# Sample projections of a hybrid layer: later column matmuls, row sums through DRAM and VectorE, spatial weights transposed one step later

## The chip, the cores and the metric

The kernel runs on one core of a Trainium2 chip. The metric is the device time of one execution in microseconds (us); the time of a kernel is the median of its runs. Each run is one whole step of the layer, from the inputs in device memory to all nine outputs there.

## What is computed

One decoder layer is applied to two groups: a prompt of 2048 tokens, and eight samples of one new token each, with their stored state. Both go through one input projection with 3856 columns, whose column groups feed three mixers: sliding-window attention (A), a chunked spatial gating unit (B) and gated linear attention (C). The mixers' outputs are gated, joined and projected back.

```python
h = rmsnorm(x, g_norm)
proj = h @ w_in_l                    # (T, 1024) @ (1024, 3856)
(qa, ka, va, ga, ub, vb, gb, qc, kc, vc, gc, lr) = split(proj)
ya = attention(qa, ka, va)           # window 128, bias, sinks; samples use stored keys
yb = ub * (spatial_w @ layernorm(vb) + spatial_b)   # in chunks of 128 tokens
yc = gla(qc, kc, vc, decay(lr))      # recurrent state per head
y = concat([ya * silu(ga), yb * silu(gb), yc * silu(gc)])
x = x + y @ w_out_l
```

The eight samples need the same `h @ w_in_l` with eight rows; this change concerns how those eight rows are made and handed on. The last keys and values of the prompt, the new keys and values of the samples, the recurrent states and the normalised `vb` rows of the samples are outputs too.

## The kernel before, in words

**Numbers and passes.** The f32 operands of the large products are split into two f16 halves (hi and lo), and each product is three f16 passes (hi hi, hi lo, lo hi) summed in PSUM.

**Stages.** The prompt is cut into 8 chunks of 256 tokens (16 tiles of 128). Stage A runs the A columns over all chunks with the attention beside them, stage B the B columns with the spatial mixing, stage C the C columns with the gated linear attention, and stage F the output projection. A *unit* is one accumulation of 24 matmuls (8 k-steps by 3 passes) into a PSUM bank of the tag `pp`: `mm_col` (L296) gives columns by tokens, `mm_tok` (L307) tokens by columns. There are four `pp` banks for units and four `mx` banks for everything else. The final projection's units have 36 matmuls (L1008).

**What a unit feeds in stage A.** Gate units: ACT writes a tanh (L486), DVE multiplies it with the bank (L487). Query units: ACT writes the hi half (L476), DVE the lo half (L477). Key and value units the same way (`unit_va` around L457). In the last chunk `unit_k` also makes the output of the last 128 keys: DVE scales the bank into `kf` (L441), PE transposes it (L443), ACT copies it and SP stores it.

**Attention beside the units.** A step is a tile and half of the heads: score matmuls (L506), DVE's bias-and-maximum (L510), small DVE steps (L520 to L524), ACT's exponentials (L538), an f16 copy by ACT (L548) into the tile `pha` and a subtraction by GpSimd (POOL, L549) into `phb`, small DVE steps (L551 to L558), two DMA transposes on SP into `pt` (L563), the products with the values on PE (L578), two DVE multiplications (L583, L585) and a store on SP (L588). Tiles `pha` and `phb` have one buffer each, the tag `yy` has six, `pt` two.

**Splitting the weights.** A slice of 512 columns is loaded by SP (L164), ACT writes the hi half, DVE the lo half (L204). The slices for stage B are split in stage A.

**The order.** Steps are emitted in the order of a clock: every k-step of a unit advances `now` by its columns divided by 2400 (so about the us at full clock), and `at(t, f)` puts a step on a list that runs when `now` reaches t. `weave`, `merge` and `spread` place steps between the units of stages B, C and F. On top of this the Tile framework's scheduler chooses each engine's order; it has to hold what is written by one engine and read by another, and what `tc.keep_in_program_order` names.

**A sample projection** (`sample_proj`, L322) takes one slice of the weights. 16 matmuls (`four_way`, L320) of 32 columns by up to 512 fill four groups of 32 partitions; each group holds partial sums of hi and lo parts for the eight samples. ACT copies the bank, scaled, to the `yy` tile `part` (L329). The eight partial sums of each sample (four groups, hi and lo rows of `h`) must still be added, which a matmul with the selector `selg` (128 x 8, f32) does in two forms:

- *columns* (calls with `keep`, A0 and C0, and the 16 low-rank columns of A1): `part` is the stationary operand, so the result lies columns on partitions (L334, L338); DVE copies it to `scolA`, `scolC` or `slr` (L336, L339);
- *rows* (calls with `outs`): `selg` is the stationary operand (L343); ACT copies the 8 rows (L345) and SP stores them to the DRAM tile `sp_d` (L347), from which the sample steps of the mixers read much later (`sA_load`, `sC_load`, whose loads are at L1187 among others, and the output at L1045).

The calls: A1 (rows for keys and values, columns for the low rank), A0 (columns), A2 (rows) near the end of stage A, eight units of clock apart; B0, B1, B2 (rows) in chunk 2 of stage B; C0 (columns), C1, C2 (rows) in chunk 1 of stage C.

**Spatial weights.** `consts_B` (L593) runs in the last slots of chunk 0 of stage B. SP loads the weights of eight groups into `pha` and `phb` (L601), PE transposes them (L609), DVE masks them, and PE transposes the biases (L613). The first reader is `b_mix`, in chunk 1.

Other lines the text refers to: L904, a DVE reduce of stage C; L942, a load of output weights by SP in stage C.

Of the kernel before, what the change touches and what calls it, by code (L numbers as in the profile page):

```python
# [10 lines left out]
F32 = mybir.dt.float32  # L11
# [5 lines left out]
ALU = mybir.AluOpType  # L17
AX = mybir.AxisListType
# [21 lines left out]
DIN = _o  # L40
# [3 lines left out]
def hybrid_step_kernel(ctx: ExitStack, tc: tile.TileContext, I, O):  # L44
    nc = tc.nc
    V, S, G, PE, SP = nc.vector, nc.scalar, nc.gpsimd, nc.tensor, nc.sync
# [33 lines left out]
    def mbank():  # L80
        return psm.tile([128, 512], F32, tag="mx", name=nm("mx"))
# [7 lines left out]
    def w4(tag, shape, dt=F32):  # L89
        return wk.tile(shape, dt, tag=tag, name=nm(tag), bufs=WB.get(tag, 2))  # L90
# [3 lines left out]
    hs_d = dr.tile([16, DM], F16, name="hs_d")  # L94
    ys_d = dr.tile([16, DMIX], F16, name="ys_d")
    sp_d = dr.tile([NB, DIN], F32, name="sp_d")

    w_in = I["w_in"][0]
    w_out = I["w_out"][0]
# [176 lines left out]
    def at(t, *fs):  # L276
        for f in fs:
            cnt[0] += 1
            bisect.insort(EV, (t, cnt[0], f))
# [42 lines left out]
    def sample_proj(name, n, outs, keep=None):  # L322
        w = SL[name]
        inv = INVI[name]
        m = n % 128
        ps = mbank()
        four_way(ps, min(n, 512), lambda i: hs[:, i // 2, :], [w[:, i % 2, i // 2, 0:n] for i in range(16)])
        part = w4("yy", [128, 512])
        S.activation(out=part[:, :n], in_=ps[:, :n], func=AF.Copy, scale=inv)  # L329
        if keep is not None or m:  # L330
            p2 = mbank()
            cols = range(n // 128) if keep is not None else ()
            for ct in cols:
                PE.matmul(p2[:, ct * 8:ct * 8 + 8], part[:, ct * 128:(ct + 1) * 128], selg, start=True, stop=True)  # L334
            if keep is not None:
                V.tensor_copy(out=keep.rearrange("p a b -> p (a b)"), in_=p2[:, 0:32])  # L336
            if m:
                PE.matmul(p2[:m, 32:40], part[:, n - m:n], selg, start=True, stop=True)  # L338
                V.tensor_copy(out=slr, in_=p2[:m, 32:40])  # L339
        if outs:  # L340
            p3 = mbank()
            nf = n - m
            PE.matmul(p3[:8, :nf], selg, part[:, :nf], start=True, stop=True)  # L343
            row = w4("yy", [8, 512])
            S.copy(row[:, :nf], p3[:8, :nf])  # L345
            for a, b, off in outs:
                SP.dma_start(out=sp_d[:, off:off + b - a], in_=row[:, a:b])  # L347

    BM = {}

# [242 lines left out]
    def consts_B():  # L593
        t = one.tile([128, 2048], F32, tag="bm", name="phB")
        wsT["w"] = t[:, 0:1024].rearrange("p (a b) -> p a b", a=8)
        wsT["g"] = t[:, 1024:1536]
        wsT["b"] = t[:, 1536:2048]
        wsT["bs"] = sm.tile([128, 8], F32, tag="bs", name="bs", bufs=1)
        ws = [w4("pha", [128, 4, 128]), w4("phb", [128, 4, 128])]
        for q in range(2):  # L600
            SP.dma_start(out=ws[q], in_=I["spatial_w"][0, 4 * q:4 * q + 4].rearrange("h i j -> i h j"))  # L601
        SP.dma_start(out=wsT["g"], in_=I["chunk_ln_g"].partition_broadcast(128).rearrange("p a b -> p (a b)"))
        SP.dma_start(out=wsT["b"], in_=I["chunk_ln_b"].partition_broadcast(128).rearrange("p a b -> p (a b)"))
        bsr = small([8, 128])
        SP.dma_start(out=bsr, in_=I["spatial_b"][0])
        for q in range(2):
            ps = mbank()
            for i in range(4):
                PE.transpose(ps[:, i * 128:(i + 1) * 128], ws[q][:, i, :], ident)  # L609
            V.tensor_tensor(out=wsT["w"][:, 4 * q:4 * q + 4, :], in0=ps.rearrange("p (a b) -> p a b", a=4),  # L610
                            in1=upm.unsqueeze(1).to_broadcast([128, 4, 128]), op=ALU.mult)
        ps = mbank()
        PE.transpose(ps[:, 0:8], bsr, ident[:8, :8])  # L613
        V.tensor_copy(out=wsT["bs"], in_=ps[:, 0:8])
# [670 lines left out]
    def merge(*seqs):  # L1285
        n = max((len(s) for s in seqs), default=0)
        out = [[] for _ in range(n)]
        for s in seqs:
            for i, fs in enumerate(s):
                out[i * n // len(s)] += fs  # L1290
        return out

    def spread(steps, at, total):
        out = [[] for _ in range(total)]
        for s, i in zip(steps, at):
            out[min(i, total - 1)].append(s)
        return out

    if True:
# [88 lines left out]
        for c in range(NCH):  # L1388
            units = [unit_vb(c, 0), unit_vb(c, 1), unit_gate("B1", hgB, c, 0), unit_gate("B1", hgB, c, 1),
                     unit_ub(c, 0), unit_ub(c, 1)]  # L1390
            extra = []
            if c == 0:
                for f, d in zip(prB[2][1:], (0, 9, 10.5, 12)):
                    at(now[0] + d, f)
                V.tensor_scalar(out=hgB, in0=INVI["B1"], scalar1=0.5, scalar2=None, op0=ALU.mult)
                side = [[]] * 11 + [[lambda: V.tensor_scalar(out=cB, in0=hgB, scalar1=INVI["B2"], scalar2=None, op0=ALU.mult),
                                     consts_B]]
            else:
                side = mixB(c - 1)
            if c == 1:  # L1400
                extra = spread([sA_load, sA_kT], [1, 4], 6)
            if c == 2:
                extra = spread([sA_soft, sA_pv,
                                lambda: sample_proj("B0", 512, [(0, 512, OFF["vb"])]),
                                lambda: sample_proj("B1", 512, [(0, 512, OFF["gb"])]),
                                lambda: sample_proj("B2", 512, [(0, 512, OFF["ub"])])], [0, 2, 3, 4, 5], 6)
            if c == 3:
                extra = spread([sB], [2], 6)
            if c == 4:
                extra = spread([load_wup, alloc_C, c0_up(0), c0_up(1), c0_exp(0), c0_exp(1), c0_ln((0, 1)), c0_scan(0), c0_scan(1)],  # L1410
                               [0, 0, 0, 1, 2, 3, 4, 5, 5], 6)
            if c == 5:
                extra = spread([c0_up(2), c0_up(3), c0_exp(2), c0_exp(3), sC_la, c0_ln((2, 3)), sC_ln, c0_scan(2),
                                c0_scan(3), sC_exp],
                               [0, 1, 2, 2, 3, 4, 4, 5, 5, 5], 6)
            if c == 6:
                extra = spread([prC[0][0]], [3], 6)
            if c == 7:
                extra = spread(prC[0][1:] + [prC[1][0]], [1, 2, 3, 4, 4], 6)
            weave(units, merge(side, extra) or [[]])  # L1420

        for c in range(NCH):
# [21 lines left out]
                    lambda: sample_proj("C1", 512, [(0, 512, OFF["vc"])]),  # L1444
                    lambda: sample_proj("C2", 512, [(0, 512, OFF["gc"])])], [1, 4, 6], 8))
            if c == 2:
                extra = merge(extra, spread([sC_load], [0], 8))
            if c == 3:
                extra = merge(extra, spread([sC_mix, sC_state], [0, 2], 8))
            if c in (1, 2, 3):  # L1450
# [74 lines left out]
```

## Time and profile before

| | |
|---|---|
| median of 3 runs | 1192.56 us (1190.77 to 1195.8) |
| the profiled execution | 1196.03 us |
| its span, first to last instruction | 1194.3 us |
| VectorE (DVE) busy | 677.2 us, 57% |
| ScalarE (ACT) busy | 480.9 us, 40% |
| GpSimd (POOL) busy | 72.9 us, 6% |
| granted TensorE clock, mean | 0.99 |

A row of the timeline has: start in us from the span's start, busy us, engine, line, operation, output and inputs, shapes, and a count; a bracket is the idle time of that engine just before, and what ended it. SPq is SP's DMA queue. A row of the windows view has the stretch and its length, then the busy time (and the number of instructions) of PE, PE's weight load, DVE, ACT and POOL, then the granted clock, the busy share of the DMA engines, and the GB/s that they moved. A group row has the line, engine, operation and tiles, a count, the shortest, median and longest time in ns, and where in the span it lies.

### The profile page before, as it was taken

Reading aid. Unit: us, or ns where it says so; the run is one execution under the profiler, and the core shown is the slowest. Engines: PE = TensorE matmul, PEld = TensorE weight load, DVE = VectorE, ACT = ScalarE, POOL = GpSimd, SP = SyncE. Lnnn points to the kernel's source line nnn. Section 1 sums busy time; section 2 is a strip of 40 time slices with the busy share of each in tenths; the row PEclk is TensorE's granted clock in tenths of the full one; section 3 lists DMA queues with packets and bytes.
Section 4 is the critical chain, followed back from the end, with each engine's and each line's share of the span. In section 5 each row is a group of like instructions: output and inputs, shape, how many; then the busy total and the mean of one; then the engine's idle time right before and its main releaser. Section 6 shows DMA issues by size and latency. Waiting matters only on the chain.

```text
span 1194.3 us, 19595 instructions
## 1 busy us (share of the span) xinstructions
PE 1136.0 (95%) x7637; PEld 663.4 (56%) x7637; DVE 677.2 (57%) x2229; ACT 480.9 (40%) x967; POOL 72.9 (6%) x49
## 2 busy tenths in 40 slices
PE   4997899997998999999999999999999999999997
PEld 3756577775654544444465567566665543444443
DVE  5887866657686355576284355645545643544442
ACT  7776755565771021552265411412212131322220
POOL 0012222222210000000000000000000000000000
PEclk9998999998999999999999999999999999999999
DMA  9579954534454002000054521220114446766641
GB/s 274 158 129 199 190 150 89 75 78 104 112 138 116 18 22 85 8 18 18 18 186 121 207 55 31 94 89 18 54 44 129 121 124 159 208 160 164 165 124 54
DMA packets 196913, 128.63 MB, mean 108 GB/s; under 512 B 155922, under 2 KB 170395, under 8 KB 196819
## 3 DMA queue, kind: packets, MB, share of 16 engines
q1 hardware_dynamic: 196818, 127.36, 41.4%
q8 instruction: 60, 0.98, 0.3%
q14 instruction: 35, 0.28, 0.1%
HBM read 66.36 MB, written 23.63 MB: 75 GB/s over the span
## 4 chain that ended last, share of the span: by engine, by line
PE 59%; DVE 3%; DMA 3%; ACT 2%; issue 1%; SPq 1%; POOL 0%; DVEq 0%; ACTq 0%
PE pp L307 31%; PE pp L1008 14%; PE pp L296 6%; DMA hb<-sl 2%; PE mx L671 1%; PE mx L867 1%; PE mx L849 1%; PE mx L873 1%; PE mx L881 1%; PE mx L320 1%; DMA sl<-y_d 1%; ACT sl L977 1%; SPq L989 1%; DVE sl L997 1%; DMA sl<-in_w_in_dram 0%
## 5 line engine op out<-in xcount | busy, mean ns | idle before, releaser
L307 PE MATMUL pp<-sl,hb 128*128 128x512 f16 x2304 | 516.9, 380 | 1.3 <-DVE qk L477 1.3
L307 PEld LDWEIGHTS <-hb 128*128 128x128 f16 x2688 | 250.2, 99 | 268.8 <-issue 12.5
L1008 PE MATMUL pp<-hb,hb 128*128 128x512 f16 x1152 | 251.2, 380 | 2.5 <-DMA hb<-sl 2.5
L1008 PEld LDWEIGHTS <-hb 128*128 128x128 f16 x1152 | 111.7, 98 | 140.3 <-DMA hb<-sl 5.4
L296 PE MATMUL pp<-hb,sl 128*128 128x256 f16 x1536 | 178.8, 275 | 8.7 <-DVE yy L487 8.6
L296 PEld LDWEIGHTS <-sl 128*128 128x128 f16 x1536 | 149.3, 98 | 31.9 <-issue 11.5
L549 POOL TENSOR_TENSOR phb<-Lp,pha 128x1024 f16<-128x1024 f32 (+1 forms) x32 | 66.5, 2079 | 288.0 <-ACT pha L548 270.9
L1011 DVE SCALAR_TENSOR_TENSOR sl<-pp,finv,sl 128x512 f32<-128x512 f32 x32 | 23.9, 748 | 85.8 <-PE pp L1008 85.8
L486 ACT ACTIVATE yy<-pp,scal 128x512 f32<-128x512 f32 x48 | 32.5, 679 | 81.5 <-PE pp L307 65.4
L994 ACT ACTIVATE sl<-sl 128x1024 f32<-128x1024 f32 (+1 forms) x16 | 16.9, 1056 | 116.8 <-DVE sl L1011 114.8
L538 ACT ACTIVATE Lp<-Lp,sm 128x256 f32<-128x256 f32 (+1 forms) x128 | 62.3, 488 | 0.2
L510 DVE CUSTOM_DVE_ANT_0 Lp<-mx,BM,scal 128x256 f32<-128x256 f32 (+1 forms) x128 | 54.7, 472 | 4.0 <-PE mx L506 3.4
L487 DVE SCALAR_TENSOR_TENSOR yy<-yy,pp 128x512 f32<-128x512 f32 x48 | 32.8, 682 | 42.2 <-ACT yy L486 42.2
L623 ACT ACTIVATE kk<-pp,invs 128x512 f32<-128x512 f32 x16 | 10.9, 683 | 93.3 <-PE pp L307 93.3
L477 DVE SCALAR_TENSOR_TENSOR qk<-pp,qk 64x256 f16<-64x256 f32 x64 | 26.9, 422 | 37.6 <-ACT qk L476 36.8
L978 DVE SCALAR_TENSOR_TENSOR sl<-sl,ch 128x1536 f16<-128x1536 f32 (+1 forms) x17 | 30.9, 1817 | 20.3 <-ACT sl L977 20.3
L977 ACT ACTIVATE sl<-sl,ch 128x1536 f16<-128x1536 f32 (+1 forms) x17 | 26.8, 1575 | 32.1 <-DVE ch L144 32.1
L637 DVE BATCH_NORM_STATS2 sm<-kk 128x6 f32<-128x512 f32 x16 | 11.1, 691 | 50.2 <-ACT kk L623 50.2
L204 DVE SCALAR_TENSOR_TENSOR sl<-sl,gs,sl 128x512 f16<-128x512 f32 x48 | 36.1, 813 | 3.6 <-ACT sl L203 3.3
L506 PE MATMUL mx<-kk,qk 128*128 128x256 f16 (+1 forms) x256 | 33.4, 271 | 4.7 <-DVE sm L510 4.7
L307 PE MATMUL pp<-s,hb 128*128 128x144 f16 x384 | 31.9, 246 | 5.9 <-DMA hb<-sl 3.6
L548 ACT CAST pha<-Lp 128x1024 f16<-128x1024 f32 (+1 forms) x32 | 32.4, 1012 | 5.1 <-DMA pt<-pha 4.7
(320 smaller groups left out, 1234.1 us busy)
## 6 DMA issues: line engine op xcount, KB each, us to landing
sl<-in_x_prompt_dram SPq DMA_DIRECT2D x32, 512.0 KB
sl<-in_w_in_dram SPq DMA_DIRECT2D x24, 512.0 KB
sl<-in_w_out_dram SPq DMA_DIRECT2D x6, 2048.0 KB
sl<-y_d SPq DMA_DIRECT2D x16, 768.0 KB
y_d<-yy SPq DMA_DIRECT2D x32, 256.0 KB
out_dram<-sl SPq DMA_DIRECT2D x15, 512.0 KB
hb<-in_w_in_dram SPq DMA_DIRECT2D x8, 512.0 KB
y_d<-Lp SPq DMA_DIRECT2D x8, 512.0 KB
```

What stands on the lines that cost most here:

```text
L204: V.scalar_tensor_tensor(out=lo, in0=src, scalar=gk, in1=hi, op0=ALU.mult, op1=ALU.subtract)
L296: PE.matmul(ps[:m, :CT], w[:, wl, k, c0:c0 + m], h[:, hl, k, :], start=(n == 0), stop=(n == 23))
L307: PE.matmul(ps[:, :n_], h[:, hl, k, j * 128:(j + 1) * 128], w[:, wl, k, c0:c0 + n_], start=(n == 0), stop=(n == 23))
L486: S.activation(out=g, in_=ps, func=AF.Tanh, scale=hg)
L487: V.scalar_tensor_tensor(out=g, in0=g, scalar=1.0, in1=ps, op0=ALU.add, op1=ALU.mult)
L506: PE.matmul(pv[:, hh, :], Qt[c][:, h // 2, h % 2, j * 128:(j + 1) * 128], Kt[c][:, 2 * hb + hl, ko:ko + W], start=(hl == 0), stop=(hl == 1))
L510: V.tensor_tensor_reduce(out=L[:, i, :], in0=pv[:, hh, :], in1=BM["t"][:, 4 * hb + i, 256 - W:256], scale=cS, scalar=-3e38, op0=ALU.add, o ...
L538: S.activation(out=L[:, i, :], in_=L[:, i, :], func=AF.Exp, bias=nb[:, i:i + 1], accum_out=den[:, i:i + 1])
L548: S.copy(P[0], L)
L549: G.tensor_tensor(out=P[1], in0=L, in1=P[0], op=ALU.subtract)
L977: S.activation(out=d["h"][:, 0, :], in_=d["y"], func=AF.Copy, scale=s)
L1008: PE.matmul(ps, d["yT"][:, hl, k, :], wo[k // 2][:, wl, k % 2, cs], start=(n == 0), stop=(n == 35))
```

## The change

Three things are changed, and the order on the engines follows.

1. The column matmuls and DVE's copies of their results are no longer emitted in the projection itself, but 6 on the emission clock later, and the matmuls are named to `keep_in_program_order`.
2. The row-sum matmul, ACT's copy and the store are gone. `part` (128 rows) is stored to a new DRAM tile `sq_d`; four loads, one for each group of 32 rows, bring it back so that a block of 64 columns of one sample stands on a partition of its own, with its eight partial sums side by side; a DVE reduce, emitted 8 on the clock after the projection, adds the eight; the result is stored to `sp_d`.
3. The transposes of `consts_B` become a step of their own, `consts_B2`, placed one unit later (first slot of chunk 1 of stage B); the loads stay where they were. `sC_load`, which reads `sp_d`, moves from the first to the second slot of chunk 2 of stage C.

```diff
@@ -94,6 +94,7 @@
     hs_d = dr.tile([16, DM], F16, name="hs_d")
     ys_d = dr.tile([16, DMIX], F16, name="ys_d")
     sp_d = dr.tile([NB, DIN], F32, name="sp_d")
+    sq_d = dr.tile([DIN // 16 + 8, 128 * 16], F32, name="sq_d")
 
     w_in = I["w_in"][0]
     w_out = I["w_out"][0]
@@ -327,24 +328,38 @@
         four_way(ps, min(n, 512), lambda i: hs[:, i // 2, :], [w[:, i % 2, i // 2, 0:n] for i in range(16)])
         part = w4("yy", [128, 512])
         S.activation(out=part[:, :n], in_=ps[:, :n], func=AF.Copy, scale=inv)
-        if keep is not None or m:
+
+        def columns():
             p2 = mbank()
             cols = range(n // 128) if keep is not None else ()
-            for ct in cols:
-                PE.matmul(p2[:, ct * 8:ct * 8 + 8], part[:, ct * 128:(ct + 1) * 128], selg, start=True, stop=True)
+            todo = [(p2[:, ct * 8:ct * 8 + 8], part[:, ct * 128:(ct + 1) * 128]) for ct in cols]
+            if m:
+                todo.append((p2[:m, 32:40], part[:, n - m:n]))
+            for o, a in todo:
+                tc.keep_in_program_order(PE.matmul(o, a, selg, start=True, stop=True))
             if keep is not None:
                 V.tensor_copy(out=keep.rearrange("p a b -> p (a b)"), in_=p2[:, 0:32])
             if m:
-                PE.matmul(p2[:m, 32:40], part[:, n - m:n], selg, start=True, stop=True)
                 V.tensor_copy(out=slr, in_=p2[:m, 32:40])
+
+        if keep is not None or m:
+            at(now[0] + 6, columns)
         if outs:
-            p3 = mbank()
-            nf = n - m
-            PE.matmul(p3[:8, :nf], selg, part[:, :nf], start=True, stop=True)
-            row = w4("yy", [8, 512])
-            S.copy(row[:, :nf], p3[:8, :nf])
-            for a, b, off in outs:
-                SP.dma_start(out=sp_d[:, off:off + b - a], in_=row[:, a:b])
+            (a, nf, off), = outs
+            nb = nf // 64
+            base = off * 128
+            SP.dma_start(out=bass.AP(tensor=sq_d.tensor, offset=base, ap=[[nf, 128], [1, nf]]), in_=part[:, :nf])
+            t = w4("yy", [8 * nb, 8, 64])
+            for g in range(4):
+                SP.dma_start(out=t[:, 2 * g:2 * g + 2, :],
+                             in_=bass.AP(tensor=sq_d.tensor, offset=base + 32 * g * nf, ap=[[64, 8 * nb], [8 * nf, 2], [1, 64]]))
+            red = small([8 * nb, 64])
+
+            def add():
+                V.tensor_reduce(out=red, in_=t.rearrange("p q j -> p j q"), axis=AX.X, op=ALU.add)
+                SP.dma_start(out=bass.AP(tensor=sp_d.tensor, offset=off, ap=[[DIN, 8], [64, nb], [1, 64]]), in_=red)
+
+            at(now[0] + 8, add)
 
     BM = {}
 
@@ -603,6 +618,10 @@
         SP.dma_start(out=wsT["b"], in_=I["chunk_ln_b"].partition_broadcast(128).rearrange("p a b -> p (a b)"))
         bsr = small([8, 128])
         SP.dma_start(out=bsr, in_=I["spatial_b"][0])
+        wsT["ws"], wsT["bsr"] = ws, bsr
+
+    def consts_B2():
+        ws, bsr = wsT["ws"], wsT["bsr"]
         for q in range(2):
             ps = mbank()
             for i in range(4):
@@ -1398,7 +1417,7 @@
             else:
                 side = mixB(c - 1)
             if c == 1:
-                extra = spread([sA_load, sA_kT], [1, 4], 6)
+                extra = spread([consts_B2, sA_load, sA_kT], [0, 1, 4], 6)
             if c == 2:
                 extra = spread([sA_soft, sA_pv,
                                 lambda: sample_proj("B0", 512, [(0, 512, OFF["vb"])]),
@@ -1444,7 +1463,7 @@
                     lambda: sample_proj("C1", 512, [(0, 512, OFF["vc"])]),
                     lambda: sample_proj("C2", 512, [(0, 512, OFF["gc"])])], [1, 4, 6], 8))
             if c == 2:
-                extra = merge(extra, spread([sC_load], [0], 8))
+                extra = merge(extra, spread([sC_load], [1], 8))
             if c == 3:
                 extra = merge(extra, spread([sC_mix, sC_state], [0, 2], 8))
             if c in (1, 2, 3):
```

On PE the column matmuls of A0 move behind the transpose of the last keys (L443; in the changed kernel's numbering L458). Before, they stood in the middle of a unit of `unit_va`; `mx_4202` is their bank, `yy_4200` is `part`, and some 180 rows lie between the two pieces:

```order
L307 LDWEIGHTS hb_3037
L307 MATMUL pp_4179<-s_14_156,hb_3037 128x144
L334 MATMUL mx_4202<-selg,yy_4200 128x8 x4
L307 LDWEIGHTS hb_3037
...
L296 MATMUL pp_4429<-hb_3037,sl_227 128x256
L443 MATMUL mx_4342<-ident,sm_4340 128x128
L578 LDWEIGHTS pt_4018
L578 MATMUL mx_4366<-vt_3014,pt_4018 128x64
```

Now the unit of `unit_va` runs through, and the four matmuls stand behind the transpose and the 24 products with the values, right ahead of the next projection (A2):

```order
L297 MATMUL pp_4434<-hb_3038,sl_228 128x256
L458 MATMUL mx_4341<-ident,sm_4339 128x128
L593 LDWEIGHTS pt_4018
L593 MATMUL mx_4365<-vt_3015,pt_4018 128x64
...
L593 MATMUL mx_4365<-vt_3061,pt_4018 128x64
L339 MATMUL mx_4396<-selg,yy_4203 128x8 x4
L321 LDWEIGHTS hs
L321 MATMUL mx_4438<-sl_478,hs 32x512
```

What moved: the four matmuls of A0, past the rest of this unit of `unit_va`, a second one, the unit of `unit_k` with two pairs of scores, a query unit, the first matmuls of another, the transpose and the 24 products. The transpose itself stands where it stood.

On DVE, in stage A between the weight splits (L204) and the gate eviction (L487), the order before was this; the `sm` and `rc` tiles belong to the attention's soft-max, `mx_4202` is the bank of A0's columns:

```order
L204 SCALAR_TENSOR_TENSOR sl_3929<-sl_3636,gs_4094,sl_3929 128x512 x4
L551 TENSOR_TENSOR sm_4136<-sm_4061,sm_4062 128x4
L583 TENSOR_TENSOR yy_4173<-mx_4148,rc_3854 128x256
L557 RECIPROCAL sm_4139<-sm_4136 128x4
L520 TENSOR_TENSOR sm_4217<-sm_4103,sinkb 128x4
L585 TENSOR_TENSOR yy_4173<-yy_4173,yy_3574 128x256
L558 TENSOR_SCALAR rc_4138<-sm_4139,scal 128x4
L487 SCALAR_TENSOR_TENSOR yy_4176<-yy_4176,pp_4072 128x512
L336 COPY scolA<-mx_4202 128x32
```

Now A1's low-rank copy stands ahead of these steps and A1's reduce (L359, of the tile that the four loads fill) among them, before the gate eviction (now L502); the copy to `scolA` is gone from here:

```order
L205 SCALAR_TENSOR_TENSOR sl_3930<-sl_3637,gs_4094,sl_3930 128x512 x4
L343 COPY slr<-mx_4129 16x8
L566 TENSOR_TENSOR sm_4139<-sm_4061,sm_4062 128x4
L598 TENSOR_TENSOR yy_4176<-mx_4151,rc_3855 128x256
L572 RECIPROCAL sm_4142<-sm_4139 128x4
L359 TENSOR_REDUCE sm_4005<-yy_4000 32x64
L573 TENSOR_SCALAR rc_4141<-sm_4142,scal 128x4
L600 TENSOR_TENSOR yy_4176<-yy_4176,yy_3575 128x256
L502 SCALAR_TENSOR_TENSOR yy_4179<-yy_4179,pp_4072 128x512
```

What moved: one reduce came in ahead of the gate eviction, and one copy went behind it and later.

On SP, at the same place, A1's store of rows stood ahead of two pairs of attention transposes; `pha` and `phb` are the f16 halves, `pt` the transposed ones:

```order
L347 DMA sp_d<-yy_4003 8x256
L563 DMA_TRANSPOSE pt_4018<-pha_4009 128x8x128
L563 DMA_TRANSPOSE pt_4018<-phb_4010 128x8x128
L588 DMA y_d<-yy_3892 128x512
L1045 DMA out_dram<-sp_d 8x128 x2
L563 DMA_TRANSPOSE pt_4142<-pha_4132 128x8x128
L563 DMA_TRANSPOSE pt_4142<-phb_4133 128x8x128
```

Now the store of `part` stands there, the loads behind the first pair, and the store of the sums behind the second:

```order
L351 DMA sq_d<-yy_3997 128x256
L578 DMA_TRANSPOSE pt_4018<-pha_4009 128x8x128
L578 DMA_TRANSPOSE pt_4018<-phb_4010 128x8x128
L354 DMA yy_4000<-sq_d 32x2x64 x4
L603 DMA y_d<-yy_3893 128x512
L578 DMA_TRANSPOSE pt_4145<-pha_4135 128x8x128
L578 DMA_TRANSPOSE pt_4145<-phb_4136 128x8x128
L360 DMA sp_d<-sm_4005 8x4x64
L1064 DMA out_dram<-sp_d 8x128 x2
```

What moved: two output copies of `sp_d` (L1045, now L1064) from between the pairs to behind the second, and five DMAs came in. Up to the first sample projection, about 270 us into the span, the order of every engine is the same in both kernels.

## The prediction

> **What bounds the kernel now.** The page first: TensorE (PE) is busy for 95% of the span, so time is won only where PE waits or has less to do.
>
> ```profile
> span 1194.3 us, 19595 instructions
> PE 1136.0 (95%) x7637; PEld 663.4 (56%) x7637; DVE 677.2 (57%) x2229; ACT 480.9 (40%) x967; POOL 72.9 (6%) x49
> ```
>
> PE's timeline comes next, at the first two sample projections (A1, A0). The bracket is PE's wait and who ended it.
>
> ```profile
> 266.18 1.47 PE L307 MATMUL pp<-sl,hb 128*128 128x512 f16 x6
> 271.45 0.21 PE L338 MATMUL mx<-selg,yy 128*16 128x8 f32 x2 [3.80 <-ACT yy L329]
> 271.51 0.59 PE L343 MATMUL mx<-yy,selg 128*8 128x256 f32 x2
> 272.04 0.87 PE L578 MATMUL mx<-vt,pt 128*128 128x64 f16 x24
> ...
> 286.75 1.88 PE L334 MATMUL mx<-selg,yy 128*128 128x8 f32 x8 [3.44 <-ACT yy L329]
> 288.48 3.76 PE L307 MATMUL pp<-s,hb 128*128 128x144 f16 x30
> ...
> 300.22 0.33 PE L443 MATMUL mx<-ident,sm 128*128 128x128 f32 x1 [0.53 <-DVE sm L441]
> ```
>
> Twice PE stands at a selector matmul whose input ACT has not yet written (L329). After the second stall the granted clock, the eighth column of the windows view (behind POOL), falls to half; after the first it does not:
>
> ```profile
> 272.00:276.00 4.00, 4.00 (x41) 2.29 (x41) 2.21 (x6) 2.54 (x11) 1.13 (x1) 1.00 0.01 2
> 284.00:288.00 4.00, 1.25 (x6) 1.25 (x7) 2.99 (x10) 2.69 (x5) 0.00 (x0) 0.84 0.37 70
> 288.00:292.00 4.00, 4.00 (x33) 4.00 (x34) 3.32 (x9) 1.47 (x6) 0.00 (x0) 0.50 0.00 0
> 292.00:296.00 4.00, 4.00 (x32) 3.32 (x31) 1.22 (x6) 2.30 (x6) 1.27 (x1) 0.81 0.73 184
> ```
>
> The last three rows lose 4 x (0.16 + 0.50 + 0.19) = 3.4 us.
>
> **Part 1: the row-sum matmuls (L343) go.** Three of the seven stand in stage B, two in stage C, where PE has no waits around them:
>
> ```profile
> 430.76 1.03 PE L343 MATMUL mx<-yy,selg 128*8 128x512 f32 x2
> 431.72 4.49 PE L307 MATMUL pp<-sl,hb 128*128 128x512 f16 x20
> ```
>
> From start to next start is 0.96 us, so five give 4.8 us, all on PE's path. A2's, the same shape, gives 0.96 in stage A, A1's 272.04 - 271.51 = 0.53.
>
> What takes their place runs elsewhere: per projection one store of 256 KB (A1: 128), four loads, a reduce on VectorE (DVE), and a store. A reduce over as many elements exists:
>
> ```profile
> L904 DVE TENSOR_REDUCE ch<-yy x16: 677/683/689, 666.0 to 940.6; 128x4 f32<-128x512 f32 x16
> ```
>
> So 0.69 us each; off the path where DVE idles, on it in stage A (below). ACT loses its seven copies. The reduce waits for two DRAM trips in a row, and DVE, an in-order queue, holds all behind it meanwhile. The slowest trip of the trace stands in stage C, a 16 KB store queued behind a 2 MB load, and L1187 had to wait for it:
>
> ```profile
> 677.12 0.37 SPq L942 DMA_DIRECT2D sl<-in_w_out_dram  x1
> 679.78 0.30 SPq L347 DMA_DIRECT2D sp_d<-yy  x1
> 684.91 0.74 SPq L1187 DMA_DIRECT2D sm<-sp_d  x1
> ```
>
> 5.1 us. Two such trips and four issues of up to 0.7 us are some 13 us, against a reduce emitted 8 us after the projection: at worst DVE stands 5 us. PE's four projection banks cover that in B and C, where a unit takes 24 x 0.216 = 5.2 us (4.49 over 20 above, less its last tail). I take 0; uncovered at both C places it costs 10 at most. Below zero it cannot go: nothing waits on these sums but sample steps.
>
> **Part 2: the column matmuls (L334, L338) move about 6 us later.** Both stalls go, with A1's row sum and the clock loss: 3.80 + 3.44 + 0.53 + 3.4 = 11.2 us, if nothing else is late. But DVE is next. PE must pass L443, a transpose of what DVE writes at L441, and it already waits 0.53 there. DVE from the gate eviction before it:
>
> ```profile
> 276.49 0.69 DVE L487 SCALAR_TENSOR_TENSOR yy<-yy,pp 128x512 f32<-128x512 f32 x1 [2.21 <-ACT yy L486]
> ```
> ```profile
> 299.81 0.35 DVE L441 TENSOR_SCALAR sm<-pp,invs 128x128 f32<-128x128 f32 x1
> ```
> ```profile
> 276.49:300.16 23.67, 19.76 (x181) 15.80 (x178) 17.54 (x59) 13.61 (x33) 5.19 (x4) 0.86 0.60 145
> ```
>
> Of these 23.67 us DVE works 17.54. Its order is kept up to L441 but for the small copies and the added reduce (0.69), so L441 cannot end sooner than 18.2 us after L487 starts. And L487 moves little: ACT was busy without a gap until 271.4, then follows DVE's soft-max steps; of its queue ahead of L486 only a copy goes:
>
> ```profile
> 274.06 0.34 ACT L345 COPY yy<-mx 8x256 f32<-8x256 f32 x1
> ```
>
> That is L487 at 276.2 and L441's end at 294.4; with small gaps between dependent steps 294.5, against 300.16 now. Gain at L443: 5.7, not 11.2. PE's own work would bring it there at about 300.22 - 0.53 - 11.2 - 0.9 (L334 now stands behind) = 287.6, so it waits some 7 us, at PSUM banks and at L443. One more row can shift DVE: a four-column step beside GpSimd's subtraction:
>
> ```profile
> 271.13 2.03 DVE L558 TENSOR_SCALAR rc<-sm,scal 128x4 f32<-128x4 f32 x1
> ```
> ```profile
> 270.96 2.16 POOL L549 TENSOR_TENSOR phb<-Lp,pha 128x1024 f16<-128x1024 f32 x1 [11.11 <-ACT pha L548]
> ```
>
> The next L549 comes sooner once its ACT step no longer waits for transposes:
>
> ```profile
> 279.59 1.04 ACT L548 CAST pha<-Lp 128x1024 f16<-128x1024 f32 x1 [3.13 <-DMA pt<-pha]
> ```
>
> It would then fall beside DVE's short steps behind L487, where now it falls beside larger ones: between 0 and 2.1 us later. I take 0 and keep 2.1 for the range. [...]
>
> So long a wait also invites the half clock. Its price lies between 0 (after the 3.80 us stall) and 3.4 (after the 3.44 us one); I take 2.2, nearer the second since the wait is longer. [...]
>
> Behind L443 the four column matmuls now cost what they cost at full clock, and A2's row sum (0.96) is gone:
>
> ```profile
> 659.42 1.06 PE L334 MATMUL mx<-selg,yy 128*128 128x8 f32 x8
> 660.33 2.02 PE L296 MATMUL pp<-hb,sl 128*128 128x256 f16 x17
> ```
>
> 0.96 - 0.91 = 0.05. Stage A: 5.7 - 2.2 + 0.05 = 3.5 us (C0's columns only change place.)
>
> SP, the DMA queue, is moved too. Before, it stood at L347 for ACT's copy, with a transpose behind it:
>
> ```profile
> 274.43 0.29 SPq L347 DMA_DIRECT2D sp_d<-yy  x1
> 274.84 1.23 SPq L563 DMA_TRANSPOSE pt<-pha  x1
> ```
>
> Now the store goes once L329 is done, near 271.5, so those transposes start some 3 us earlier; this is the 3.13 us that L548 waited. The four loads behind them wait for the store to land, and the next transposes stand behind the loads. The order shows that tile pt_4018, filled at 274.84, is read right behind L443, 25 us later: a hold of a few us costs nothing.
>
> **Part 3: spatial weights.** The transposes (L609) are emitted one unit later; the loads stay.
>
> ```profile
> 365.49 0.66 PE L609 MATMUL mx<-ident,pha 128*128 128x128 f32 x4 [2.25 <-DMA pha<-in_spatial_w_dram]
> 367.05 0.63 PE L609 MATMUL mx<-ident,phb 128*128 128x128 f32 x4 [0.91 <-DMA phb<-in_spatial_w_dram]
> ```
>
> PE gets a unit of 24 matmuls and 24 of attention in between, over 5.2 us against 3.16 of waiting: 3.16 us gained. What reads the transposed weights comes three units later. If DVE, which ran behind there, stops the moved attention step instead, 0.
>
> **The sum.** 4.8 + 3.5 + 3.16 = 11.5 us. The profiled execution took 1196.03 us (1.7 beside its span) and comes to 1184.5; it lies 3.5 above the median, 1192.56, which comes to 1181.0.
>
> **The rivals.** *Nothing is late behind the stalls:* stage A gives 11.2 + 0.05, and the sum is 19.2: 1173.4. For it: PE's waits are named after ACT alone. Against: the 17.54 us of DVE work. *The cover fails in stage A:* DVE is held by GpSimd (2.1), the clock costs its full 3.4, and the reduce for A1 stands in front of the gate eviction until its loads land. Stage A then gives about 0 and the sum is 8.0 or less: 1184.6 to 1189. *The change turns slower:* the DRAM trips stop DVE or SP for so long that PE runs out of banks. Four banks of 5.2 us leave some 15 us from the last eviction; the reduce must be over 20 us later than its emission, at several of seven places, and eat 11.5 + 6 = 17.5 us: three places with 6 us each, 1199. Against it: 5.1 us is the slowest trip found.
>
> **How the numbers follow.** Forecast (1177 to 1184.5, its unknowns being the clock, 0 to 3.4, and GpSimd, 0 to 2.1): 0.58. Nothing late (1171 to 1177): 0.18. Cover fails: 0.2, of which two thirds end above 1186.6, the bound of 0.5% (6.0 us), about what a measurement of this kernel can tell from no change. Slower: 0.04. The range runs from 1172.5 to 1188.0 and leaves out the outer parts of the rivals. Faster 0.83, same 0.13, slower 0.04.
>
> **What would show it.** Right: no wait on L329 in PE's list; a wait for DVE L441 at the transpose of 4 to 7 us, perhaps with half clock behind it; PE 4.8 us shorter in B and C; no wait at the spatial transposes; the reduce beginning without PE waiting behind it. Wrong: PE passing that transpose without a wait (the first rival), or PE waiting in B or C on banks that DVE frees behind a reduce (the last).

## The result and the profile after

The changed kernel takes 1186.11 us (median of 6 runs, 1183.47 to 1187.67) against 1193.84 for the kernel before on the same occasion (6 runs): a ratio of 0.9933, interval 0.991 to 0.9955, so 5 to 11 us faster. A second set of runs gave 0.9932 (0.9916 to 0.9947). The forecast of 1181.0 was 5 us too low; the range holds the result, which lies where the prediction had put "the cover fails".

The page's head, then PE's timeline where the first two sample projections stand (compare the rows at 271 to 300 us of before):

```profile
span 1183.4 us, 19624 instructions
PE 1127.1 (95%) x7623; PEld 661.8 (56%) x7623; DVE 681.8 (58%) x2236; ACT 477.1 (40%) x960; POOL 72.6 (6%) x49
```
```profile
273.43 0.21 PE L339 MATMUL mx<-selg,yy 128*16 128x8 f32 x2
273.57 1.47 PE L308 MATMUL pp<-sl,hb 128*128 128x512 f16 x6
276.02 0.86 PE L593 MATMUL mx<-vt,pt 128*128 128x64 f16 x24 [0.98 <-DVE ch L188]
...
277.90 1.05 PE L321 MATMUL mx<-sl,hs 128*32 128x512 f16 x16 [0.83 <-DVE sm L525]
...
285.19 3.55 PE L297 MATMUL pp<-hb,sl 128*128 128x256 f16 x31
293.78 0.48 PE L458 MATMUL mx<-ident,sm 128*128 128x128 f32 x1 [5.03 <-DVE sm L456]
294.05 1.49 PE L593 MATMUL mx<-vt,pt 128*128 128x64 f16 x24
295.34 1.86 PE L339 MATMUL mx<-selg,yy 128*128 128x8 f32 x8
```

The two stalls at ACT's copy are gone. In their place stands one wait of 5.03 us at the transpose of the last keys, and what follows it runs at half clock: the 24 products take 1.49 us (0.86 a little earlier). The windows view has the clock in its eighth column:

```profile
288.00:292.00 4.00, 0.74 (x7) 0.41 (x5) 3.78 (x16) 2.46 (x5) 2.83 (x3) 1.00 0.90 278
292.00:296.00 4.00, 2.22 (x29) 2.17 (x29) 2.84 (x9) 3.19 (x12) 0.21 (x1) 0.54 0.75 275
296.00:300.00 4.00, 4.00 (x28) 2.29 (x28) 0.56 (x3) 0.92 (x2) 0.00 (x0) 0.50 0.87 192
300.00:304.00 4.00, 4.00 (x27) 3.10 (x26) 0.45 (x2) 1.45 (x3) 2.12 (x1) 0.68 0.29 97
```

DVE from the gate eviction to what the transpose waits for, and that stretch as one window (DVE is the fifth column, 18.08 of 18.52 us):

```profile
275.20 0.69 DVE L502 SCALAR_TENSOR_TENSOR yy<-yy,pp 128x512 f32<-128x512 f32 x1 [2.02 <-ACT yy L501]
...
282.15 1.01 DVE L359 TENSOR_REDUCE sm<-yy 32x64 f32<-32x512 f32 x1
283.09 0.21 DVE L573 TENSOR_SCALAR rc<-sm,scal 128x4 f32<-128x4 f32 x1
...
293.37 0.35 DVE L456 TENSOR_SCALAR sm<-pp,invs 128x128 f32<-128x128 f32 x1
```
```profile
275.20:293.72 18.52, 11.89 (x151) 10.21 (x150) 18.08 (x60) 13.23 (x33) 5.19 (x4) 0.96 0.53 144
```

At the spatial transposes (L628) PE passes without a bracket:

```profile
362.92 3.40 PE L308 MATMUL pp<-sl,hb 128*128 128x512 f16 x15
366.16 0.60 PE L628 MATMUL mx<-ident,pha 128*128 128x128 f32 x4
366.60 0.60 PE L628 MATMUL mx<-ident,phb 128*128 128x128 f32 x4
```

The reduces, and the worst place for them, C1 in stage C, on DVE and on SP's queue. The store of partial sums stands behind a 2 MB load again: store to loads 9.1 us, loads to reduce 4.1, and DVE holds its queue for 4.41 us (3.35 at C2):

```profile
L359 DVE TENSOR_REDUCE sm<-yy 64x64 f32<-64x512 f32 x6 | 6.2, 1042 | 9.0 <-DMA yy<-sq_d 9.0
```
```profile
682.09 1.04 DVE L359 TENSOR_REDUCE sm<-yy 64x64 f32<-64x512 f32 x1 [4.41 <-DMA yy<-sq_d]
```
```profile
668.27 0.37 SPq L961 DMA_DIRECT2D sl<-in_w_out_dram  x1
668.85 0.34 SPq L351 DMA_DIRECT2D sq_d<-yy  x1
677.98 2.54 SPq L354 DMA_DIRECT2D yy<-sq_d  x4
```

To see where the time went, the trace of each kernel is cut at the same events: the starts of the gate evictions on ACT (L486, after L501) that stand at 245.35, 331.19, 384.83, 643.56 and 729.55 us in before, and the last output eviction. Two executions of each kernel, in us (the second of before is the run before_again below, the second of after is whole_again):

| stretch | before | after | gain (means) | forecast |
|---|---|---|---|---|
| to 245 (same order in both) | 245.35, 244.94 | 244.31, 243.38 | 1.3 | 0 |
| 245 to 331: sample projections of stage A | 85.84, 84.32 | 83.60, 83.06 | 1.75 | 3.5 |
| 331 to 385: end of A, spatial weights | 53.64, 55.23 | 50.55, 50.55 | 3.9 | 3.16 |
| 385 to 644: stage B | 258.73, 258.72 | 255.53, 255.54 | 3.2 | 2.88 |
| 644 to 730: stage C, its first two chunks | 85.99, 86.09 | 84.33, 83.91 | 1.9 | 1.92 |
| 730 to the last eviction | 456.39, 456.17 | 456.98, 456.78 | -0.6 | 0 |

The changed stretches and the rest behind them give 10.2 us in these four traces, the medians 7.7 and 8.5. The profiled executions of before (1196.03, 1195.56 us) lie above its medians, those of after (1185.16, 1183.1) below; the traces are read for the places, the ratio for the size.

### The profile page after: what moved, and what is told of

Same layout as the page of the kernel before. It is cut to its first block, busy times and chain, and to the rows that moved or that the text cites. A ratio compares the mean times of both kernels' runs of the same rounds, so it can differ in the third digit from the quotient of the medians.

```text
span 1183.4 us, 19624 instructions
## 1 busy us (share of the span) xinstructions
PE 1127.1 (95%) x7623; PEld 661.8 (56%) x7623; DVE 681.8 (58%) x2236; ACT 477.1 (40%) x960; POOL 72.6 (6%) x49
## 4 chain that ended last, share of the span: by engine, by line
PE 58%; DMA 5%; DVE 4%; ACT 3%; issue 1%; SPq 1%; DVEq 0%; ACTq 0%
PE pp L308 31%; PE pp L1027 13%; PE pp L297 6%; DMA hb<-sl 2%; PE mx L886 1%; PE mx L690 1%; PE mx L868 1%; ACT sl L996 1%; DMA sq_d<-yy 1%; PE mx L892 1%; PE mx L900 1%; DMA sl<-in_w_out_dram 1%; DMA sl<-y_d 1%; SPq L1008 1%; DVE sl L1016 1%
## 5 line engine op out<-in xcount | busy, mean ns | idle before, releaser
L501 ACT ACTIVATE yy<-pp,scal 128x512 f32<-128x512 f32 x48 | 32.5, 680 | 84.9 <-PE pp L308 62.0
L502 DVE SCALAR_TENSOR_TENSOR yy<-yy,pp 128x512 f32<-128x512 f32 x48 | 32.7, 682 | 38.1 <-ACT yy L501 38.0
```

What stands on the lines that cost most here:

```text
L501: S.activation(out=g, in_=ps, func=AF.Tanh, scale=hg)
L502: V.scalar_tensor_tensor(out=g, in0=g, scalar=1.0, in1=ps, op0=ALU.add, op1=ALU.mult)
```

## The experiments

**The whole and its three parts.** The same kernel again, and before with one part of the change each: the columns' `at(now[0] + 6, columns)`; the DRAM path in place of the row-sum matmul, with the later `sC_load`; `consts_B2`. All on one chip. Each part is one of the three numbered items of the change.

> The whole change once more, beside its three parts on the same chip. Theory (the sum of the prediction with the sizes of the trace after): stage A 2.2 us (PE reaches the transpose of the last keys 5.4 us sooner, less 3.2 us of half clock behind it), the spatial wait 3.1, stage B 3.2, stage C 1.7: about 10 us under before. Rival, from the medians so far: the change is worth 7.7 us and the profile of before happened to be some 3 us slow, so about 8.

> Before, with the column matmuls and their copies 6 later; row sums still by matmul at once. Theory (VectorE's queue sets when PE passes the transpose of the last keys): A1's row sum still stands 3.8 us at ACT's copy, A0's 3.44 us stall goes, PE then waits 3 to 5 us at the transpose, with half clock behind it: 2 to 3 us faster than before, nothing in stages B and C. Rival (each stall of PE is worth its own length): 3.44 us and the 3.4 us of clock behind it, 6.8 us faster, with no wait at the transpose.

> Before, with the row sums through DRAM and VectorE; columns as before. Theory (row sums are PE time in stages B and C, covered everywhere else): 4.9 us in B and C and 0.96 for A2, less up to 1.0 for the reduce ahead of the transpose of the last keys: 4.9 to 5.9 us faster. Both stalls at ACT's copy stay. Rival (the two DRAM trips hold VectorE, and PE's banks run out): 0 to 2 us faster, with waits of PE for VectorE behind a reduce.

> Before, with the transposes of the spatial weights one unit later. Theory (what follows them has slack): both waits of PE at these transposes, 3.16 us, go: 3.1 us faster. Rival (VectorE or the attention step that is moved up stops PE instead): 0 to 1 us, with a new wait between 350 and 385 us.

| kernel | ratio to before (interval) | 245-331 | 331-385 | 385-644 | 644-730 |
|---|---|---|---|---|---|
| whole_again | 0.9932 (0.9916-0.9947) | 83.06 | 50.55 | 255.54 | 83.91 |
| columns_alone | 1.0015 (0.9998-1.0031) | 86.79 | 53.41 | 258.72 | 85.81 |
| sums_alone | 0.9987 (0.9974-1.0001) | 83.71 | 56.51 | 255.52 | 85.08 |
| spatial_alone | 0.9961 (0.9946-0.9975) | 84.02 | 50.07 | 258.72 | 85.99 |

The whole repeats with 8.5 us, nearer to its rival's 8 than to the 10 of the traces. The parts seem not to add up to it: by medians the columns alone are 2.4 us slower (1195.16 against 1192.78; the interval touches no change), the sums 1.3 and the spatial part 4.6 us faster. The three ratios multiply to 0.9963 against 0.9932, a gap about as wide as the noise of the four intervals together, so this is likely and not shown. Theory and rival on the columns both fall. Alone they gain nothing, because A1's row sum still stands at ACT's copy, and then the transpose waits, with half clock behind it (0.50 and 0.67):

```profile
269.86 1.02 PE L348 MATMUL mx<-yy,selg 128*8 128x256 f32 x2 [3.84 <-ACT yy L329]
295.73 0.40 PE L448 MATMUL mx<-ident,sm 128*128 128x128 f32 x1 [2.58 <-DVE sm L446]
```
```profile
296.00:300.00 4.00, 4.00 (x45) 3.44 (x47) 1.79 (x5) 1.59 (x6) 0.00 (x0) 0.50 0.65 172
300.00:304.00 4.00, 4.00 (x26) 1.45 (x17) 0.00 (x0) 1.08 (x2) 0.00 (x0) 0.67 0.57 140
```

The sums alone come out at the rival's size without its mechanism. They gain their 3.2 us in stage B and 1.0 in C, with no stop behind a reduce to speak of (DVE itself stands 4.19 and 4.14 us there in C; PE's only wait for DVE that is not in the list of before's waits there is 0.6 us), and lose 2.9 (against the first trace of before) or 1.3 (against the second) between 331 and 385 us. There PE stands 2.09 and 1.99 us at the spatial transposes (2.25 and 0.91 in before), and the clock falls behind them (0.36 and 0.06 of 4 us each, 1.7 us):

```profile
362.65 0.66 PE L618 MATMUL mx<-ident,pha 128*128 128x128 f32 x4 [2.09 <-DMA pha<-in_spatial_w_dram]
365.29 1.08 PE L618 MATMUL mx<-ident,phb 128*128 128x128 f32 x4 [1.99 <-DMA phb<-in_spatial_w_dram]
```
```profile
364.00:368.00 4.00, 2.71 (x9) 1.47 (x10) 3.18 (x7) 0.00 (x0) 0.00 (x0) 0.64 0.36 100
368.00:372.00 4.00, 4.00 (x39) 2.12 (x38) 0.85 (x2) 0.00 (x0) 0.00 (x0) 0.94 0.62 146
```

The second trace of before, below, has the same 1.7 us of half clock there without the sums, so at this place only about 1 us of the second wait can be put to them. The third part hides that. Its own theory holds, with more than the 3.16 us by the median (the interval takes 3.16 in): no wait is left, and the 245 to 385 stretch is 134.09 us, where before has 139.48 and 139.55.

**Before, profiled again.** Only to see how far one execution goes from the other.

> The kernel before, profiled a second time, to see how much of stage A's difference is between two executions of one order. Theory (the first profile of before was a slow one there: half clock of 3.4 us fell behind the second stall, at 286 us, and none behind the first): from 245 to 322 us in the first profile this one takes 1.5 to 2.5 us less, as the run with only the spatial part changed did. Rival: within 0.5 us of the first profile there.

The theory holds for stage A: 245 to 331 us takes 84.32 us, 1.5 less than in the first trace. There is a third execution of this order: spatial_alone has the order of before on every engine up to 365 us, and takes 84.02 us. So the first trace, from which the prediction was worked out, is the longest of three in stage A. The waits of PE and the clock behind the first of them:

```profile
271.06 0.22 PE L338 MATMUL mx<-selg,yy 128*16 128x8 f32 x2 [3.84 <-ACT yy L329]
287.42 1.06 PE L334 MATMUL mx<-selg,yy 128*128 128x8 f32 x8 [1.92 <-ACT yy L329]
298.11 0.33 PE L443 MATMUL mx<-ident,sm 128*128 128x128 f32 x1 [0.97 <-DVE sm L441]
...
363.40 0.66 PE L609 MATMUL mx<-ident,pha 128*128 128x128 f32 x4 [2.10 <-DMA pha<-in_spatial_w_dram]
365.13 0.93 PE L609 MATMUL mx<-ident,phb 128*128 128x128 f32 x4 [1.07 <-DMA phb<-in_spatial_w_dram]
```
```profile
272.00:276.00 4.00, 4.00 (x32) 2.27 (x32) 1.90 (x6) 2.43 (x10) 0.73 (x1) 0.50 0.11 20
...
364.00:368.00 4.00, 2.93 (x11) 1.44 (x11) 3.93 (x9) 0.00 (x0) 0.00 (x0) 0.66 0.53 151
368.00:372.00 4.00, 4.00 (x39) 2.06 (x38) 0.85 (x2) 0.00 (x0) 0.00 (x0) 0.91 0.66 150
```

Here the half clock falls behind the first stall, and the second stall is 1.92 us, not 3.44: with PE slow, ACT is less far behind when A0's columns come (argued from the order of events, not tried by itself). At the spatial transposes the clock falls as well (0.34 and 0.09 of 4 us, 1.7 us), which the first trace doesn't have. By chance the two differences cancel: 139.48 and 139.55 us over both stretches.

**The whole without late columns.** `sums_alone` plus `consts_B2`.

> The whole change without its late columns. Theory (late columns buy almost nothing, and the parts do not add up because the row sums through DRAM lengthen the waits at the spatial transposes by 1 us and add 1.7 us of half clock there, which the third part hides): spatial stretch as in the whole change (no wait), stages B and C as there, stage A within 1.5 us of it: 0 to 1.5 us slower than the whole change, 7 to 8.5 us faster than before. Rival (the parts simply add, 1.3 and 4.6 us, and late columns bring the missing 2.6 us in the whole change): 5.9 us faster than before.

0.993 (0.991 to 0.995), the same as the whole: the late columns buy nothing that the runs can tell, as the theory says, and the rival's 5.9 us (0.9951) lies just outside the interval. The theory's reason is not borne out, though. The ratios of sums_alone and spatial_alone multiply to 0.9948, inside this interval, and in the traces the two parts do add from 245 to 385 us as a whole: against before the sums make 0.7 us more, the spatial part 5.4 less, both together 4.5 less. What is hidden at the spatial transposes is missing again before 331 us, and 1.1 us more of the gain lies in stage C (83.99 us here, 85.08 in sums_alone). Both stalls are there again, and the transpose hardly waits; 245 to 385 us is 135.05 us (whole: 134.15 and 133.61):

```profile
268.88 0.22 PE L339 MATMUL mx<-selg,yy 128*16 128x8 f32 x2 [3.81 <-ACT yy L330]
283.47 1.06 PE L335 MATMUL mx<-selg,yy 128*128 128x8 f32 x8 [1.80 <-ACT yy L330]
295.51 0.33 PE L452 MATMUL mx<-ident,sm 128*128 128x128 f32 x1 [0.67 <-DVE sm L450]
```

**Taking the new wait away.** Four kernels built on the whole change: the transpose later; DVE's split steps out of its way; then one and two of the scale steps of the weights later too; and the last of them with the columns at once again.

```diff
 transpose_late:
-                p2 = mbank()
-                PE.transpose(p2[:, 0:128], kf, ident)
...
+                def kout():
+                    p2 = mbank()
+                    tc.keep_in_program_order(PE.transpose(p2[:, 0:128], kf, ident))
...
+                at(now[0] + 12, kout)
 splits_late:
-        for f, d in zip(LOADP["B0"] + prB[0][1:], (0, 3, 6, 9, 12, 20, 21.5, 24)):
+        for f, d in zip(LOADP["B0"] + prB[0][1:], (0, 3, 6, 9, 12, 20, 34, 36)):
 (and its DVE halves named to keep_in_program_order)
 both_late, on transpose_late:
-        for f, d in zip(prB[1][1:], (0, 8, 9.5, 11)):
+        for f, d in zip(prB[1][1:], (0, 11.5, 13, 14.5)):
 three_late, on both_late:
-                for f, d in zip(prB[2][1:], (0, 9, 10.5, 12)):
+                for f, d in zip(prB[2][1:], (0, 13, 14.5, 16)):
```

> The whole change, with the transpose of the last keys (not its input on VectorE) emitted 12 later. Theory (PE stands only at this one place, VectorE catches up while four banks cover): the 5.0 us wait and the 3.2 us of half clock behind it go, 5 to 8 us under the whole change. Rival (VectorE is behind by that much, so that PE waits for it at the next bank or score instead): the wait moves, 0 to 2 us under the whole change.

> The whole change, with the second halves of the stage B weight split (eight steps of VectorE, 0.73 to 0.78 us each, 6 us together) behind the scaling of the last keys; PE's order stays. Theory (VectorE's queue alone sets the end of that wait): the scaling ends up to 6 us sooner, PE's wait at the transpose falls from 5 us to under 1, no half clock: 5 to 8 us under the whole change. Rival (ACT's query evictions or GpSimd set it): the wait stays above 3 us and the time within 2 us of the whole change.

> The whole change with the transpose of the last keys 12 later, as in transpose_late, and with the scale step of the second stage B slice (its matmul L186 waits 5.5 us for ACT's squares in transpose_late) 3.5 later, with its split. Theory (PE meets one late helper after another, and each wait of over 3 us brings 2.7 to 3.4 us of half clock): with both out of the way the 5.5 us and the 2.7 us behind it go, 5 to 8 us under transpose_late and under the whole change. Rival (the attention steps on VectorE and ACT beside these units set the end of stage A, so the wait moves a third time, to a score bank or an eviction): within 2 us of transpose_late, with a new wait of PE of 3 to 5 us between 300 and 360 us.

> As both_late, with the scale step of the third stage B slice (its matmul L186 waits 4.7 us for ACT's squares there, with 1.7 us of half clock) 4 later, with its split. Theory (a chain of late helpers, each in PE's queue ahead of work that is ready; VectorE and ACT themselves have time to spare in stage A): that wait goes, 4 to 6 us under both_late and under the whole change. Rival (the chain of load, squares, scale and split of the stage B slices is the end that stage A runs into, and only moves where PE meets it): within 2 us of both_late, with PE waiting 3 us or more for a split half or an eviction at the start of stage B.

> As three_late, but with the column matmuls at once, as before the change. Theory (late columns save PE two waits of 3.8 and 1.9 us, and half clock behind the first, and nothing shows of it only because later waits take it back): with the later waits moved, 4 to 8 us slower than three_late. Rival (something else ends stage A at the same time whatever PE does before it): within 1.5 us of three_late.

| kernel | ratio to before (interval) | 245-331 | 331-385 | both |
|---|---|---|---|---|
| after, whole_again | 0.9933, 0.9932 | 83.60, 83.06 | 50.55, 50.55 | 134.15, 133.61 |
| transpose_late | 0.9922 (0.9902-0.9942) | 81.91 | 51.49 | 133.40 |
| splits_late | 0.9933 (0.9913-0.9954) | 82.66 | 50.60 | 133.26 |
| both_late | 0.9937 (0.9924-0.9951) | 76.32 | 57.40 | 133.72 |
| three_late | 0.9928 (0.9909-0.9947) | 77.22 | 57.43 | 134.65 |
| three_late_columns_at_once | 0.9937 (0.9918-0.9957) | 77.24 | 57.47 | 134.71 |

Each time the theory falls and the rival has the time right: no kernel is clear of the whole change, and the 5.0 us and the clock behind it come back as waits elsewhere, though not always where the rival had put them. With the transpose out of the way, PE stands at the scale step of the next slice, for ACT's squares and not for VectorE (transpose_late):

```profile
313.91 0.59 PE L186 MATMUL mx<-sm,ones 128*128 128x4 f32 x2 [5.54 <-ACT sl L180]
```

With DVE relieved of 6 us of splits the wait at the transpose falls to 3.22 us, and no further: DVE, until then without a gap, now waits for ACT's value evictions (L473; the rival had named the query evictions). And 2.23 us come back at a scale step (splits_late, PE and then DVE):

```profile
290.52 0.33 PE L460 MATMUL mx<-ident,sm 128*128 128x128 f32 x1 [3.22 <-DVE sm L458]
315.27 0.39 PE L186 MATMUL mx<-sm,ones 128*128 128x4 f32 x2 [2.23 <-ACT sl L180]
```
```profile
285.26 0.29 DVE L474 SCALAR_TENSOR_TENSOR vt<-pp,vt 128x128 f16<-128x128 f32 x1 [1.78 <-ACT vt L473]
```

With that step later as well, ACT's four squares (1.04 us each) stand ahead of a query eviction, a score matmul waits for that, and PE, some 7 us ahead by 331 us, gives it all back at the third slice's scale step (both_late):

```profile
313.76 0.39 PE L525 MATMUL mx<-kk,qk 128*128 128x256 f16 x2 [2.73 <-DVE qk L496]
...
333.12 0.59 PE L186 MATMUL mx<-sm,ones 128*128 128x4 f32 x2 [4.68 <-ACT sl L180]
```

And with all three later, a score matmul waits 3.12 us (its row of two matmuls then takes 0.61 us, 0.39 in both_late), and the split of the third slice, which the edit itself moved, is what stage B waits for, 2.0 us where the rival had said 3 or more (three_late):

```profile
314.29 0.61 PE L525 MATMUL mx<-kk,qk 128*128 128x256 f16 x2 [3.12 <-DVE qk L496]
...
346.50 0.38 PE L308 MATMUL pp<-sl,hb 128*128 128x512 f16 x1 [1.60 <-ACT sl L204]
347.29 7.46 PE L308 MATMUL pp<-sl,hb 128*128 128x512 f16 x26 [0.41 <-DVE sl L205]
```

With the columns at once (three_late_columns_at_once) it is the same to 0.1 us in the trace, although PE stands 3.78 and 1.98 us at ACT's copy again: the rival holds. No wait of PE over 0.4 us stands there between 285.83 and 348.35 us, so what late columns save three_late loses at the score matmul. Shown is that in these five kernels what PE saves at one helper is lost at the next ones: at 385 us they are within 1.1 us of the whole change's 134.15 and 133.61. That is no floor, for the next kernel comes to 132.10. Not settled is whether another placing of scale steps and splits would keep it: the last edit moved its own split too far, so it does not separate the chain of the weights from the placing.

**Without the trips.** Only the partial sums' first rows are stored, straight to `sp_d`; no loads, no reduce.

```diff
-            nb = nf // 64
...
-            at(now[0] + 8, add)
+            SP.dma_start(out=sp_d[:, off:off + nf], in_=part[0:8, :nf])
```

> The whole change without the loads, the reduce and the store of sums: the first 8 rows of the partial sums go to the DRAM tile unadded (the sum over the eight partial rows is left out). Theory (the trips cost nothing but 1.04 us of VectorE ahead of the transpose of the last keys): 0 to 1.2 us under the whole change, nothing in stages B and C. Rival (VectorE's stands of 4.4 and 3.4 us in stage C and the busier SP queue cost PE): 2 to 5 us under it.

0.9911 (0.989 to 0.9932), an interval that overlaps the whole's. In the trace 245 to 331 us takes 81.54 us, 1.5 to 2.1 less than the whole. One reduce of 1.01 us is gone from DVE's queue ahead of the transpose, and the wait there is 4.16 us, not 5.03. The half clock behind it is shorter too: by the three windows it loses 4 x (0.24 + 0.50 + 0.11) = 3.4 us, where the whole loses 4 x (0.46 + 0.50 + 0.32) = 5.1:

```profile
294.64 0.47 PE L445 MATMUL mx<-ident,sm 128*128 128x128 f32 x1 [4.16 <-DVE sm L443]
```
```profile
292.00:296.00 4.00, 1.36 (x22) 1.30 (x23) 2.85 (x12) 3.37 (x13) 0.66 (x2) 0.76 0.93 333
296.00:300.00 4.00, 4.00 (x33) 2.54 (x31) 1.33 (x4) 0.60 (x3) 0.00 (x0) 0.50 0.76 160
300.00:304.00 4.00, 4.00 (x34) 3.42 (x33) 0.71 (x2) 2.32 (x4) 2.12 (x1) 0.89 0.33 96
```

Stage B is the same to 0.01 us (255.53), C 0.2 to 0.65 us shorter (83.68). So the trips cost next to nothing where DVE idles, and the theory's place is right: the reduce ahead of the transpose costs about its own 1 us. What goes beyond the theory's 1.2 us is half clock, and with one trace it stays open whether the shorter wait or chance made that shorter. A2's reduce, the other one in the stretch, stands where DVE waits for PE and ACT before and after it.

## Why the forecast was right in sign and too large

**Row sums (4.8 us in B and C): right.** Measured 3.2 + 1.9 = 5.1. The replacement was rightly costed at nothing in B; the reduce takes 1.04 us where 0.69 was assumed from a row of other shape; DVE's hold of "at worst 5 us" was 4.41 (by some luck: C1's trip took 9.1 + 4.1 us, where 13 had been put together from 5.1, 5.1 and 2.8), covered by the banks in B and nearly so in C, where 644 to 730 us spreads from 83.7 (no trips) to 85.3 us (transpose_late) over the kernels that have the change.

**Stage A (3.5 us): the mechanism right, the size too large.** DVE's unbroken work sets the transpose: 18.5 us from the gate eviction's start, 18.2 forecast; a wait of 5.03, "4 to 7" forecast; PE there 300.22 - 293.78 - 1.04 (lead at 245 us) = 5.4 us sooner, 5.7 forecast. Two terms were mis-sized. The first is the half clock behind the wait, "I take 2.2", out of 0 to 3.4: the windows above lose 5.1 us, because half clock lasts 10 us there and not 6.8 as in the first trace of before. Of the 5.4 us only 2.2 are left at 322 us (319.11 there, 322.38 in before, less 1.04), so 3.2 went after what PE made up. That makes stage A 2.2 us, not 3.5, against the first trace. The second is what the 5.7 was counted from: L443 at 300.22 stands behind the 3.44 us stall and half clock of that one execution. Against the second trace (298.11, lead 0.63) PE is only 3.7 us sooner, and stage A gains 0.7 to 1.3 us; against spatial_alone's 84.02 it is 0.4 to 1.0. And sums_and_spatial shows that late columns can be left out at no cost that shows.

**The rival "cover fails"** gave the right time for reasons that mostly did not occur: no reduce waited for its loads ahead of the gate eviction (the row at 282.15 has no bracket). Of its three causes the clock's full price came, and of GpSimd's a part: three short DVE steps beside GpSimd's steps at 291 us (L566, L573, L537) took 0.64, 0.68 and 0.56 us, where the same lines took 0.14, 0.21 and 0.15 at 281 to 285 us with GpSimd idle; two others between them (L572, L535) took 0.18 and 0.13.

**Spatial weights (3.16 us): right in its place and too small.** 3.1 us against the first trace, 4.7 against the second, where half clock stood behind the waits. It is the part with most of the gain: alone 134.09 us for 245 to 385, the whole 134.15 and 133.61. What the whole adds to it lies in B and C.

**What stays open.** Behind 730 us the changed kernel loses 0.6 us (both traces). There PE's waits for the inputs of the final projection (`hb`, filled by a DMA; its matmuls and weight loads together) come to 9.3 and 8.7 us, before to 7.9 and 7.5; why is open. So are the traces' 10.2 us against 7.7 and 8.5 of the medians.

## What to carry to other kernels

Before a stall is priced, look at a second execution of the same order: a wait and the half clock behind it can trade places (here 3.80 us without and 3.44 us with half clock, then 3.84 us with and 1.92 us without). A stall was worth its length here only where nothing late stood behind it: three late helpers in a row (waits of 5.54, 4.68 and 3.12 us) took back what the first gave, while the waits at the end of the stretch (3.16 us, 3.1 and 4.7 gained) and plain matmul time in a stage without waits (2.88 us in B, 3.2 gained) were worth their full price. Parts of a change need not add up, so time the parts and the whole together, and look whether the gap is wider than their noise before explaining it.

## What the runs showed of the hardware

The same wait of 3.8 us at A1's matmul left the clock at full in the first trace of before (1.00 from 272 to 276 us) and halved it in the second (0.50 from 272 to 276 us) and in spatial_alone (0.51 from 268 to 272 us), all three with the same order up to there. In before_again the clock also fell at about 365 us (0.66 from 364 to 368 us), where PE had no wait over 2.10 us: two waits, 2.10 and 1.07 us, with 0.66 us of matmuls between them. What decides whether it falls is not shown. By the granted clock the half clock lasted some 3.4 us there (a loss of 1.7 us), 6.8 us behind the 3.44 us stall of the first trace (3.4), and 10 us, to about 303 us, behind the 5.03 us wait (5.1): one price for a drop does not do. The 2.7 to 3.4 us behind "each wait of over 3 us" in both_late's theory was the author's estimate; the 3.80 us wait with the clock at full is against it.
